# The last w_up tiles of each half are turned beside w_down's first row tiles

## The chip, the cores and the metric

The kernel runs on one core of a Trainium2 chip. The metric is the device time of one execution in microseconds. The timed runs of the kernel before gave 1473.55, 1473.86 and 1475.04 us.

## The reference, cut to what matters

One hybrid decoder layer on 256 tokens of width 2048, in float32. Its first part (a state-space group and an attention group behind one input projection, then an output projection) isn't touched here. The change lies in the last part, the MLP:

```
hdn = jax.nn.relu(jnp.einsum('bsd,df->bsf', u, w_up))          # u 256 x 2048, w_up 2048 x 8192
ff  = jnp.einsum('bsf,fd->bsd', hdn * hdn, w_down)             # w_down 8192 x 2048
out = h + rmsnorm(ff, norm_mlp_post)
```

## The kernel before, in words

**Halves.** The hidden width of 8192 is worked in two halves of 4096 features. Each half is made by products with w_up, column blocks of 512, two at a time (`unit(w_ups[hf], fb, ...)`), and then used as the contraction of w_down, again two column blocks of 512 at a time: `unit(w_down, 0, ...)` and `unit(w_down, 2, ...)` for half 0, the same with `w_downs[1]` for half 1. The partial sums of half 0 stay in three tiles `mw0`, `mw1`, `mw2`.

**A matrix product.** Float32 values are split in two, a rounded part `hi` (ScalarE, `split`, L148) and the rest `lo` (VectorE, L149), and a product takes three matmuls: hi x hi, hi x lo, lo x hi. `row_tiles` does this for one row tile k, 256 rows of the weight, and one column block; both blocks together take 24 matmuls. `seven` does both blocks at once for one k with seven products in place of eight, 21 matmuls, with sums of weights (`e`, `r`, L255, made by VectorE from the two raw tiles) and sums of activations (`sums_of_acts`, L394 to L397 and a split). The sums of activations of a k are made once, kept in two places of `room["sums"]` and used again by the second unit of the half. Which k goes by seven and in which order is a table (`plan`): for the first unit of half 0 the order is 0, 1, 2, 4, 3, 6, 5, 9, 7, 10, 8, 11, 12, 13 with sevens at 4, 6, 9, 10, 11, 13, and then 14 and 15; for the first unit of half 1 the first seven is k = 3.

**Turning.** The result of w_up has tokens on partitions, and w_down needs features there. At the end of each w_up unit four tiles (two blocks by two token tiles) are turned by the generator `turned`: ScalarE squares the tile (L1477) and parts its 32-bit words into 16-bit halves in `ha` (L1478), SyncE issues a DMA transpose of the halves (L1479), and after two steps of waiting ScalarE puts the halves together again (L1482) and the result is split into the activations `ah`, `al` (L148, L149). The generators wait in `beside`; `pump_beside` carries the next one a step on, once after each row tile and twice after each seven, and `drain_beside` runs all to their end. The last four turned tiles of a half are the features of w_down's k = 12 to 15.

**Memory.** Four names of the pool `hp` are used in turn: `ha` (six places of 128 x 512), `hb` (two), `wpost` (two) and `mw`. While w_up runs, `ha` holds the four tiles of 16-bit halves and a raw place, `hb` and `wpost` the results that are turned. `beside_down` gives `ha`, `hb`, `wpost` and, last, `mw1` to the sums of w_down's half 0, and `mw2` to a raw weight tile (`room["raw"]`, behind a ring of four raw tiles). In half 1 `ha` becomes three raw places behind the ring and two in `uc`, and `hb` two more places of sums; the first sums lie in `ua`. A new tile of a name may be written only when the last user of the old one is done.

**What sets the order.** The program is written as one sequence. A scheduler places each engine's instructions at build time by the program's order, by blocks of high priority (weights, splits and sums have one), by explicit lines (`split_in_line`) and by its own reckoning of when operands are ready. Each engine then runs its list strictly in order, SyncE's list of DMA issues included, so an instruction that waits holds all behind it. Pairs of rows are added on the way by DMAs that POOL issues (`pair`, L282, L283), four pairs ahead.

In this kernel the w_up loop of a half ends with `drain_beside()`, and only then come `beside_down()` (half 0) or `in_place_of_u()` and the new raw places (half 1), and the first w_down unit.

## Time and profile before

| what | value |
|---|---|
| timed runs, median | 1473.86 us (1473.55 to 1475.04) |
| the profiled execution, its own time | 1469.89 us |
| its span, first to last instruction | 1468.1 us |
| granted TensorE clock, mean over the span | 0.989 |
| TensorE, VectorE, ScalarE, POOL busy | 98%, 88%, 68%, 11% |
| DMA | 340.30 MB, 232 GB/s |

Times in the profile are microseconds from the start of the span. PE is TensorE, DVE is VectorE, ACT is ScalarE, SP (SPq its queue) is SyncE. A line such as L148 is that of the helper which issued the instruction, so the tiles' names tell more than the lines: `hi<-raw` is the split of a raw weight tile, `ah<-ha` that of a turned tile, `ha<-r` (in w_down) that of a sum of activations. A matmul's shown duration runs to its modelled end; from start to start they are closer. `ps` and `acc` are accumulators, `sh`, `sl` and `ah`, `al` the split activations.

### The profile page before, as it was taken

Reading aid. Unit: us, or ns where it says so; the run is one execution under the profiler, and the core shown is the slowest. Engines: PE = TensorE matmul, PEld = TensorE weight load, DVE = VectorE, ACT = ScalarE, POOL = GpSimd, SP = SyncE. Lnnn points to the kernel's source line nnn. Section 1 sums busy time; section 2 is a strip of 40 time slices with the busy share of each in tenths; the row PEclk is TensorE's granted clock in tenths of the full one; section 3 lists DMA queues with packets and bytes.
Section 4 is the critical chain, followed back from the end, with each engine's and each line's share of the span. In section 5 each row is a group of like instructions: output and inputs, shape, how many; then the busy total and the mean of one; then the engine's idle time right before and its main releaser. Section 6 shows DMA issues by size and latency. Waiting matters only on the chain.

```text
span 1468.1 us, 20247 instructions
## 1 busy us (share of the span) xinstructions
PE 1441.2 (98%) x6930; PEld 1209.3 (82%) x6930; DVE 1299.2 (88%) x1881; ACT 1000.9 (68%) x1407; POOL 162.4 (11%) x244
## 2 busy tenths in 40 slices
PE   9999999999999999999999999979999999979998
PEld 8888888888888888888888888858888888858886
DVE  7788888988999787699989999879889999959998
ACT  7577669675666666566666699766565898866564
POOL 0201210121111000011100111000111111101000
PEclk9999999999999999999999999989999999989999
DMA  8967666756898657688867899778888999989854
GB/s 268 281 200 223 187 184 186 230 178 193 236 265 231 186 144 229 216 248 270 266 198 236 250 312 276 192 193 240 253 250 256 262 284 264 268 206 314 240 192 164
DMA packets 201926, 340.30 MB, mean 232 GB/s; under 512 B 45616, under 2 KB 48544, under 8 KB 201824
## 3 DMA queue, kind: packets, MB, share of 16 engines
q1 hardware_dynamic: 174304, 279.72, 60.8%
q0 software_dynamic: 19648, 45.63, 15.3%
q10 hardware_dynamic: 7872, 13.68, 2.8%
q8 instruction: 54, 0.88, 0.2%
q14 instruction: 48, 0.39, 0.1%
HBM read 327.39 MB, written 49.84 MB: 257 GB/s over the span
## 4 chain that ended last, share of the span: by engine, by line
PE 69%; DMA 3%; ACT 3%; DVE 2%; issue 1%; SPq 0%; ACTq 0%; DVEq 0%
PE acc L347 9%; PE acc L349 9%; PE acc L348 9%; PE acc L435 6%; PE acc L436 6%; PE acc L437 6%; PE acc L504 4%; PE ps L347 3%; PE ps L348 3%; PE ps L349 3%; PE ps L437 2%; PE ps L436 2%; PE ps L435 2%; PE acc L507 2%; DMA hb<-ha 1%; DMA raw<-in_w_down_dram 1%
## 5 line engine op out<-in xcount | busy, mean ns | idle before, releaser
L149 DVE TENSOR_TENSOR lo<-raw,hi 128x1024 fp32r<-128x1024 f32 (+1 forms) x402 | 486.8, 1217 | 82.1 <-ACT hi L148 80.2
L148 ACT ACTIVATE hi<-raw 128x1024 fp32r<-128x1024 f32 (+1 forms) x402 | 419.4, 1049 | 199.2 <-PE acc L349 62.2
L504 PE MATMUL acc<-ua,hi 128*128 128x512 f32 x520 | 141.2, 401 | 0.0
L148 ACT ACTIVATE hi<-e 128x1024 fp32r<-128x1024 f32 x66 | 69.8, 1058 | 49.0 <-DVE e L255 41.1
L504 PEld LDWEIGHTS acc<-ua,hi 128*128 128x128 f32 x520 | 91.3, 189 | 14.0
L347 PE MATMUL acc<-hi,ua 128*128 128x512 f32 x228 | 90.1, 395 | 0.0
L348 PE MATMUL acc<-lo,ua 128*128 128x512 f32 x228 | 89.3, 391 | 0.0
L349 PE MATMUL acc<-hi,ua 128*128 128x512 f32 x228 | 89.1, 391 | 0.0
L347 PE MATMUL acc<-hi,sh 128*128 128x512 f32 x220 | 86.5, 395 | 0.0
L349 PE MATMUL acc<-hi,sl 128*128 128x512 f32 x220 | 85.8, 390 | 0.0
L348 PE MATMUL acc<-lo,sh 128*128 128x512 f32 x220 | 85.7, 389 | 0.0
L149 DVE TENSOR_TENSOR lo<-e,hi 128x1024 fp32r<-128x1024 f32 x66 | 80.4, 1219 | 3.8 <-ACT hi L148 3.2
L507 PEld LDWEIGHTS acc<-ua,lo 128*128 128x128 f32 x520 | 76.5, 190 | 8.9
L507 PE MATMUL acc<-ua,lo 128*128 128x256 f32 x520 | 78.8, 281 | 0.0
L436 PE MATMUL acc<-lo,ah 128*128 128x512 f32 x180 | 70.3, 390 | 0.0
L437 PE MATMUL acc<-hi,al 128*128 128x512 f32 x180 | 70.1, 389 | 0.0
L435 PE MATMUL acc<-hi,ah 128*128 128x512 f32 x180 | 70.1, 389 | 0.0
L504 PE MATMUL acc<-uc,hi 128*128 128x512 f32 x208 | 61.4, 405 | 0.0
L435 PE MATMUL acc<-hi,ua 128*128 128x512 f32 x137 | 53.3, 399 | 2.5 <-ACT hi L148 2.5
L436 PE MATMUL acc<-lo,ua 128*128 128x512 f32 x137 | 53.7, 392 | 0.0
L437 PE MATMUL acc<-hi,ua 128*128 128x512 f32 x137 | 53.6, 391 | 0.0
L149 DVE TENSOR_TENSOR lo<-r,hi 128x512 fp32r<-128x512 f32 x66 | 45.2, 684 | 7.9 <-ACT hi L148 7.6
(566 smaller groups left out, 3716.7 us busy)
## 6 DMA issues: line engine op xcount, KB each, us to landing
raw<-in_w_in_dram SPq DMA_DIRECT2D x154, 512.0 KB, 4.4
raw<-in_w_up_dram SPq DMA_DIRECT2D x77, 512.0 KB, 4.8
raw<-in_w_down_dram SPq DMA_DIRECT2D x69, 512.0 KB, 5.3
raw<-in_w_out_dram SPq DMA_DIRECT2D x38, 512.0 KB, 5.1
raw<-pair SPq DMA_DIRECT2D x60, 256.0 KB, 4.2
pair<-in_w_up_dram POOLq DMA_DIRECT2D x56, 256.0 KB, 5.6
pair<-in_w_down_dram POOLq DMA_DIRECT2D x52, 256.0 KB, 6.0
pair<-in_w_in_dram POOLq DMA_DIRECT2D x42, 256.0 KB, 5.8
```

The costliest lines, as they stand in the source:

```text
L148: return (nc.scalar.activation(hi, src, AF.Copy), nc.vector.tensor_tensor(lo, src, hi.bitcast(F32), op=ALU.subtract))
L149: nc.vector.tensor_tensor(lo, src, hi.bitcast(F32), op=ALU.subtract))
L347: nc.tensor.matmul(dst[:, cs], a_h[:, r, ts], hi[:, j, cs], start=begin and j == 0, stop=False)
L348: nc.tensor.matmul(dst[:, cs], a_h[:, r, ts], lo[:, j, cs], start=False, stop=False)
L349: product[t] = nc.tensor.matmul(dst[:, cs], a_l[:, r, ts], hi[:, j, cs], start=False, stop=end and j == KB - 1)
L435: nc.tensor.matmul(dst, a_h, hi[:, j], start=own and first, stop=False)
L436: nc.tensor.matmul(dst, a_h, lo[:, j], start=False, stop=False)
L437: nc.tensor.matmul(dst, a_l, hi[:, j], start=False, stop=own and last)
L504: nc.tensor.matmul(acc[f], hi[:, j, f * P:(f + 1) * P], u(k0 + j), start=k0 + j == 0, stop=False, skip_group_check=True)
L507: nc.tensor.matmul(acc[f][:, 0], lo[:, j, f * P:(f + 1) * P], u(k0 + j)[:, 0], start=False, stop=k0 + j == NK - 1, skip_group_check=True)
```

## The change

In both halves the `drain_beside()` between the w_up loop and w_down is gone. In half 0 `beside_down` now takes only `mw1`, whose two places become the first two of `room["sums"]`, and `mw2`. The rest of the memory (`ha`, `hb`, `wpost`) is taken in `more_beside_down`, which first drains, and which `unit` calls (`ready`) just before its first seven. In half 1 the same is done by `more_in_place`: drain, `ha` and `hb`, and the loads of two post-norm weights. A row tile steps `beside` on twice instead of once (`room["pace"]`) until `beside_up` sets it back to one. What each sum is kept in moves on by two places: k = 4 in `mw1`, k = 6, 9, 10 in `ha`, 11 in `hb`, 13 in `wpost`, and the sums of k = 8, made in the second unit, in `mw1` again where they were in `ha`.

```diff
--- before.py
+++ after.py
@@ -199,18 +199,23 @@
         a = hp.tile([P, 3 * KB, NB], F32, name="ha")
         room["halves"] = [a[:, i].bitcast(U16) for i in range(2 * NT)]
         room["raw"], room["turn"], room["acts"], room["chain"] = [*raws, a[:, 2 * NT:]], turn, act_u, True
+        room["pace"] = 1
         sums_of.clear()
 
     def beside_down():
 
+        m = new_mw(1, F32R)
+        room["sums"] = [m[:, t].rearrange("p (b s) -> p b s", b=2) for t in range(NT)]
+        room["raw"], room["turn"], room["acts"], room["pace"] = [mws[2]], 0, part, 2
+        sums_of.clear()
+
+    def more_beside_down():
+
+        drain_beside()
         a = hp.tile([P, 3 * KB, 2, S], F32R, name="ha")
         b = hp.tile([P, KB, 2, S], F32R, name="hb")
-        room["sums"] = [a[:, k] for k in range(3 * KB)] + [b[:, k] for k in range(KB)]
+        room["sums"] += [a[:, k] for k in range(3 * KB)] + [b[:, k] for k in range(KB)]
         room["sums"] += [hp.tile([P, 2, S], F32R, name="wpost", bufs=2) for _ in range(2)]
-        m = new_mw(1, F32R)
-        room["sums"] += [m[:, t].rearrange("p (b s) -> p b s", b=2) for t in range(NT)]
-        room["raw"], room["turn"], room["acts"] = [mws[2]], 0, part
-        sums_of.clear()
 
     def fetch_next(src, k0, c0, pair=None):
 
@@ -369,7 +374,7 @@
                 if at == n - 1 and at_end:
                     at_end(t, acc[t])
             pump(pumps)
-            pump_beside()
+            pump_beside(room.get("pace", 1))
 
     def gemm_tokens(src, c0, acts, nk, lag=0, at_end=None, pumps=1):
 
@@ -1506,11 +1511,10 @@
             unit(w_ups[hf], fb, orders[("up", hf), fb], (7,), acc, more,
                  lambda x: combine_new(room["shared"], x), 0, (up_end(fb, 0), up_end(fb + 1, 1)))
             acc, more = more, acc
-        drain_beside()
         if hf == 0:
             beside_down()
             unit(w_down, 0, orders[("down", 0), 0], (14, 15), acc, more,
-                 lambda x: combine_new(in_mw(0), x), 0, (onto(0), onto(1)))
+                 lambda x: combine_new(in_mw(0), x), 0, (onto(0), onto(1)), ready=more_beside_down)
             room["raw"], room["turn"] = [new_mw(2)], 0
             room["sums"] += room["sums"][:4]
             unit(w_down, 2, orders[("down", 0), 2], (12, 14, 15), more, acc,
@@ -1527,15 +1531,20 @@
         return at_end
 
     in_place_of_u()
-    a, b = hp.tile([P, 3 * KB, NB], F32, name="ha"), hp.tile([P, KB, 2, S], F32R, name="hb")
     in_u = room["raw"]
-    room["raw"] = [*in_u, *(a[:, k:k + KB] for k in range(0, 3 * KB, KB))]
-    room["sums"] += [b[:, k] for k in range(KB)]
-    room["chain"] = True
-    for n in range(2):
-        load_wpost(norm_mlp_post, n)
+    room["chain"], room["pace"] = True, 2
+
+    def more_in_place():
+
+        drain_beside()
+        a, b = hp.tile([P, 3 * KB, NB], F32, name="ha"), hp.tile([P, KB, 2, S], F32R, name="hb")
+        room["raw"] = [*in_u, *(a[:, k:k + KB] for k in range(0, 3 * KB, KB))]
+        room["sums"] += [b[:, k] for k in range(KB)]
+        for n in range(2):
+            load_wpost(norm_mlp_post, n)
+
     unit(w_downs[1], 0, orders[("down", 1), 0], (14, 15), acc, more,
-         lambda x: combine_onto(0, x), 0, (complete(0), complete(1)))
+         lambda x: combine_onto(0, x), 0, (complete(0), complete(1)), ready=more_in_place)
     room["chain"] = False
 
     def onto_and_h(more):
```

The lines of code after the first hunk are 5 higher in the new kernel, those from the MLP's last part on up to 9. In half 1 no engine's list changes. Three places in half 0:

TensorE at the first seven of w_down, before. `hi_9262`, `hi_9267`, `hi_9271` and `hi_9275` are the four split weight tiles of k = 4, `hi_9310` and `hi_9327` those of row tile 3, `hi_9354`, `hi_9359`, `hi_9363`, `hi_9367` those of k = 6; the numbers tell instances of a name apart.

```order
L437 MATMUL ps_8013<-hi_9262,sl_80 128x512
L435 MATMUL ps_8015<-hi_9275,sh_79 128x512
L436 MATMUL ps_8015<-lo_9276,sh_79 128x512
L437 MATMUL ps_8015<-hi_9275,sl_80 128x512
L347 MATMUL ps_8013<-hi_9310,sh_79 128x512
L347 MATMUL ps_8015<-hi_9310,sh_79 128x512
...
L437 MATMUL ps_8013<-hi_9354,sl_80 128x512
L435 MATMUL acc_8010<-hi_9267,ha_9131 128x512
L436 MATMUL acc_8010<-lo_9268,ha_9131 128x512
L437 MATMUL acc_8010<-hi_9267,ha_9131 128x512
```

And now:

```order
L442 MATMUL ps_8013<-hi_9262,sl_80 128x512
L440 MATMUL acc_8010<-hi_9267,mw1_9113 128x512
L441 MATMUL acc_8010<-lo_9268,mw1_9113 128x512
...
L442 MATMUL acc_8014<-hi_9271,mw1_9113 128x512
L440 MATMUL ps_8015<-hi_9275,sh_79 128x512
L441 MATMUL ps_8015<-lo_9276,sh_79 128x512
L442 MATMUL ps_8015<-hi_9275,sl_80 128x512
L352 MATMUL ps_8013<-hi_9310,sh_79 128x512
...
L440 MATMUL ps_8015<-hi_9367,sh_79 128x512
L441 MATMUL ps_8015<-lo_9368,sh_79 128x512
L440 MATMUL acc_8010<-hi_9359,ha_9247 128x512
L441 MATMUL acc_8010<-lo_9360,ha_9247 128x512
```

The 12 matmuls of k = 4 on its sums stood behind row tile 3 and the first matmuls of k = 6, and read `ha`. They now read `mw1` and come right after the first six of k = 4. The first matmuls that read `ha` are those of k = 6.

ScalarE at the same place, before:

```order
L148 ACTIVATE hi_9271<-raw_9255 128x1024
L1482 ACTIVATE ha_7892<-hb_7889 128x2x512 x2
L148 ACTIVATE hi_9275<-r_9259 128x512
L148 ACTIVATE ah1_3798<-ha_7892 128x4x128 x2
L1482 ACTIVATE ha_7892<-wpost_7890 128x2x512
L1482 ACTIVATE ha_7892<-wpost_7891 128x2x512
L148 ACTIVATE hi_9310<-raw_9308 128x1024
L148 ACTIVATE hi_9327<-mw2_6211 128x1024
L148 ACTIVATE hi_9354<-raw_9343 128x1024
L148 ACTIVATE ah1_3798<-ha_7892 128x4x128 x2
L148 ACTIVATE hi_9359<-e_9350 128x1024
L148 ACTIVATE hi_9363<-raw_9347 128x1024
```

And now:

```order
L1483 ACTIVATE ha_7892<-wpost_7891 128x1024
L148 ACTIVATE hi_9271<-raw_9255 128x1024
L1487 ACTIVATE ha_7892<-hb_7889 128x2x512 x2
L148 ACTIVATE hi_9275<-r_9259 128x512
L148 ACTIVATE ah1_3798<-ha_7892 128x4x128 x2
L1487 ACTIVATE ha_7892<-wpost_7890 128x2x512
L148 ACTIVATE hi_9310<-raw_9308 128x1024
L148 ACTIVATE ah1_3798<-ha_7892 128x4x128
L148 ACTIVATE hi_9327<-mw2_6211 128x1024
L1487 ACTIVATE ha_7892<-wpost_7891 128x2x512
L148 ACTIVATE hi_9354<-raw_9343 128x1024
L148 ACTIVATE ah1_3798<-ha_7892 128x4x128
```

The split of k = 4's sums into `mw1` is new ahead of these rows; the second copy from `wpost` (L1487 now) has moved behind the splits of row tile 3, and the three writes of `ha` in a row are one, later on.

VectorE where the last turned tile is split (`al1`), before:

```order
L255 TENSOR_TENSOR e_9350<-raw_9343,raw_9347 128x512
L149 TENSOR_TENSOR al1_3799<-ha_7892,ah1_3798 128x4x128
L255 TENSOR_TENSOR e_9350<-e_9350,raw_9347 128x512
L149 TENSOR_TENSOR lo_9355<-raw_9343,hi_9354 128x1024
L255 TENSOR_TENSOR r_9351<-e_9350,raw_9343 128x512
L149 TENSOR_TENSOR lo_9360<-e_9350,hi_9359 128x1024
L394 TENSOR_TENSOR r_9392<-ah0_4884,al0_4885 128x512
L149 TENSOR_TENSOR lo_9364<-raw_9347,hi_9363 128x1024
L149 TENSOR_TENSOR al1_3799<-ha_7892,ah1_3798 128x4x128
L149 TENSOR_TENSOR ha_9131<-r_9209,ha_9131 128x512
```

And now:

```order
L260 TENSOR_TENSOR e_9350<-raw_9343,raw_9347 128x512
L260 TENSOR_TENSOR e_9350<-e_9350,raw_9347 128x512
L149 TENSOR_TENSOR lo_9355<-raw_9343,hi_9354 128x1024
L260 TENSOR_TENSOR r_9351<-e_9350,raw_9343 128x512
L149 TENSOR_TENSOR lo_9360<-e_9350,hi_9359 128x1024
L149 TENSOR_TENSOR lo_9364<-raw_9347,hi_9363 128x1024
L149 TENSOR_TENSOR lo_9368<-r_9351,hi_9367 128x512
L399 TENSOR_TENSOR r_9392<-ah0_4884,al0_4885 128x512
L149 TENSOR_TENSOR al1_3799<-ha_7892,ah1_3798 128x4x128
L400 TENSOR_TENSOR r_9393<-r_9392 128x256
L149 TENSOR_TENSOR lo_9403<-raw_9400,hi_9402 128x1024
L149 TENSOR_TENSOR ha_9247<-r_9301,ha_9247 128x512
```

The last `al1` stood behind the low part of `hi_9363`; it now stands behind `lo_9368` as well, and one write of `ha` follows two steps after it.

SyncE's queue, before:

```order
L162 DMA raw_9343<-in_w_down_dram 128x2x512
L1479 DMA_TRANSPOSE hb_7889<-ha_7892 128x8x128 x2
L157 DMA raw_9347<-pair1_90 128x512
L158 DMA raw_9347<-in_w_down_dram 128x512
L1479 DMA_TRANSPOSE wpost_7890<-ha_7892 128x8x128
L1479 DMA_TRANSPOSE wpost_7891<-ha_7892 128x8x128
```

And now:

```order
L162 DMA raw_9343<-in_w_down_dram 128x2x512
L1484 DMA_TRANSPOSE hb_7889<-ha_7892 128x8x128 x2
L1484 DMA_TRANSPOSE wpost_7890<-ha_7892 128x8x128
L157 DMA raw_9347<-pair1_90 128x512
L158 DMA raw_9347<-in_w_down_dram 128x512
L1484 DMA_TRANSPOSE wpost_7891<-ha_7892 128x8x128
```

The first `wpost` transpose has moved ahead of the two loads of k = 6's second block.

## The prediction

> **What bounds the kernel now.** I read the page first, for the span and TensorE's share of it, and then the waits of TensorE, longest first.
>
> ```profile
> span 1468.1 us, 20247 instructions
> PE 1441.2 (98%) x6930; PEld 1209.3 (82%) x6930; DVE 1299.2 (88%) x1881; ACT 1000.9 (68%) x1407; POOL 162.4 (11%) x244
> PE ps L435 <- ACT hi L148: 5.0, 2, 3.7
> PE ps L347 <- ACT hi L148: 4.8, 2, 2.5
> PE acc L435 <- ACT hi L148: 4.4, 2, 2.5
> PE acc L435 <- ACT ha L148: 3.8, 1, 3.8
> ```
>
> TensorE is busy 98% of the span. Its four largest waits (total, times, longest) add up to 18.0 us, and none of them is for an idle resource: each is for a ScalarE split. Busy time by stretch (stretch, length, then PE, PEld, DVE, ACT, POOL, granted clock, DMA share, GB/s) places them: one stall begins after 953 us, where w_down begins in the first half, another at 1300, where it begins in the second half, and between them TensorE has no gap.
>
> ```profile
> 960.00:980.00 20.00, 14.56 (x49) 11.26 (x50) 14.44 (x20) 11.20 (x14) 2.16 (x3) 0.77 0.66 169
> 980.00:1000.00 20.00, 20.00 (x90) 16.58 (x89) 19.71 (x27) 11.62 (x13) 1.36 (x2) 1.00 0.75 223
> 1000.00:1020.00 20.00, 20.00 (x90) 16.57 (x89) 19.08 (x25) 12.45 (x16) 2.72 (x4) 1.00 0.84 244
> 1300.00:1320.00 20.00, 11.35 (x33) 7.43 (x32) 9.62 (x13) 11.76 (x16) 0.55 (x1) 0.76 0.69 194
> ```
>
> The timeline of TensorE through the first stall (start, duration, engine, line, operands, and in brackets the idle time and its releaser):
>
> ```profile
> 953.05 0.39 PE L437 MATMUL ps<-hi,sl 128*128 128x512 f32 x1
> 957.18 0.79 PE L435 MATMUL ps<-hi,sh 128*128 128x512 f32 x1 [3.74 <-ACT hi L148]
> 961.66 1.22 PE L347 MATMUL ps<-hi,sh 128*128 128x512 f32 x2 [2.54 <-ACT hi L148]
> 973.09 0.80 PE L435 MATMUL acc<-hi,ha 128*128 128x512 f32 x1 [3.78 <-ACT ha L148]
> 982.03 0.39 PE L347 MATMUL ps<-hi,sh 128*128 128x512 f32 x1
> 987.48 0.39 PE L435 MATMUL acc<-hi,ah 128*128 128x512 f32 x1
> ```
>
> By the order of instructions 953.28 to 987.48 holds 84 matmuls: 3 left of the seven of k = 4, its 12 on sums, 24 of row tile 3, 6 + 12 + 3 of the seven of k = 6, and 24 of row tile 5. The last 24 run from 982.03 to 987.48, 0.227 us each. At that rate 84 take 19.1 us; they take 34.2. So 15.1 us are lost, 10.1 of them in the three waits and 5.0 to a lower granted clock (0.77 in that stretch) after them.
>
> **What the waits are for.** ScalarE and SyncE's queue at that place (the last row is the page's, with the median us to landing):
>
> ```profile
> 946.19 5.69 SPq L1479 DMA_TRANSPOSE hb<-ha  x2
> 952.05 0.46 SPq L157 DMA_DIRECT2D raw<-pair  x1
> 953.08 3.86 SPq L1479 DMA_TRANSPOSE wpost<-ha  x2
> 947.33 1.04 ACT L1478 ACTIVATE ha<-wpost 128x1024 uint16<-128x1024 uint16 x1
> 952.95 1.35 ACT L1482 ACTIVATE ha<-hb 128x1024 uint16<-128x1024 uint16 x1 [1.73 <-DMA hb<-ha]
> 955.31 1.34 ACT L1482 ACTIVATE ha<-hb 128x1024 uint16<-128x1024 uint16 x1 [1.01 <-DMA hb<-ha]
> 956.52 0.60 ACT L148 ACTIVATE hi<-r 128x512 fp32r<-128x512 f32 x1
> 957.03 1.13 ACT L148 ACTIVATE ah<-ha 128x512 fp32r<-128x512 f32 x2
> 958.17 2.54 ACT L1482 ACTIVATE ha<-wpost 128x1024 uint16<-128x1024 uint16 x2
> 960.58 1.03 ACT L148 ACTIVATE hi<-raw 128x1024 fp32r<-128x1024 f32 x1
> 972.41 1.15 ACT L148 ACTIVATE ha<-r 128x512 fp32r<-128x512 f32 x2 [1.95 <-DVE al L149]
> raw<-pair SPq DMA_DIRECT2D x60, 256.0 KB, 4.2
> ```
>
> Wait one (3.74 us): the split of the sum weights `hi<-r` stands behind two copies that wait for the transposes. Wait two: the split of row tile 3 stands behind four more steps of the drain, the last two 2.54 us together. Wait three: the sums of k = 4 live in `ha`, which is free only when the last `al<-ha` of the drain is done.
>
> **The change, part by part.** *The first sums move to `mw1`.* Its 12 matmuls now stand ahead of wait one, and need nothing of the drain. They fill 953.28 + 12 x 0.227 = 956.0. `hi<-r` itself does not move: the two `hb` transposes still land where they did, so TensorE restarts at 957.18, after 1.2 us instead of 3.9. Its price on ScalarE is one 128x512 split (0.60) ahead of the `wpost` copies, which falls into the 1.73 us in which ScalarE waits for the transposes; on VectorE its 0.6 us falls into the wait for `hi<-r`. Both hide there, and would cost 0.6 us of wait one without it.
>
> *One `wpost` copy goes behind the split of row tile 3.* That split starts 1.2 us earlier (half of 2.54, the pair being pipelined), at 959.4, and TensorE has it at 960.45 instead of 961.66. *On SyncE* one transpose passes the two loads of k = 6's second block: it starts at 952.05, not 953.08, and the loads go 1.3 us later (of the 3.86 on two transposes the first takes a third). At 4.2 us from issue to landing they are there by 958, and VectorE reads them first at 963.9; nothing waits. A transpose that reaches the head of the queue before its copy on ScalarE is done would hold every load behind it, but that copy (947.33, now 0.5 later) is done at 949.
>
> *The third wait.* No longer the sums of k = 4 but those of k = 6 wait for `ha`, and the last `al` stands further back on VectorE. Rows for its steps:
>
> ```profile
> 963.92 0.69 DVE L255 TENSOR_TENSOR e<-raw 128x512 f32<-128x512 f32 x1
> 964.52 0.68 DVE L149 TENSOR_TENSOR al<-ha,ah 128x512 fp32r<-128x512 f32 x1
> 982.40 1.22 DVE L149 TENSOR_TENSOR lo<-mw,hi 128x1024 fp32r<-128x1024 f32 x1
> 983.53 0.68 DVE L255 TENSOR_TENSOR r<-e,mw 128x512 f32<-128x512 f32 x1
> ```
>
> From start to start a 128x1024 step costs 1.13 and a 128x512 step 0.60. From the split at 960.45 VectorE has five of the first kind and seven of the second up to and with the last `al` (the two `e` and the sums' subtraction included): 5.7 + 4.2 + 0.1 for one dependent pair = 10.0, so 970.45. The write of `ha` on ScalarE (0.63) gives 971.2. Is TensorE there by then? The second half has had this very order all along, so its rows tell how TensorE gets through row tile 4:
>
> ```profile
> 1301.72 0.51 PE L435 MATMUL ps<-hi,sh 128*128 128x512 f32 x1 [1.31 <-ACT hi L148]
> 1305.42 0.80 PE L347 MATMUL ps<-hi,sh 128*128 128x512 f32 x1 [2.23 <-ACT hi L148]
> 1306.68 0.80 PE L348 MATMUL ps<-lo,sh 128*128 128x512 f32 x1 [0.46 <-DVE lo L149]
> 1310.59 0.40 PE L348 MATMUL ps<-lo,sh 128*128 128x512 f32 x1
> 1313.58 0.39 PE L349 MATMUL acc<-hi,sl 128*128 128x512 f32 x1
> ```
>
> There 24 matmuls take 1305.42 to 1313.81, 8.4 us, the nine from 1306.68 on at 0.43 each. So TensorE ends row tile 3 at 968.85, runs 8 more matmuls of k = 6 until 970.65, waits 0.55 us for `ha` (3.78 before), does 12 + 1 until 974.15 and row tile 5 until 979.6. Before it was 987.48. **The gain is 7.9 us.** At full clock TensorE would only reach the same wait earlier (960.45 + 1.25 for `lo` + 31 x 0.227 = 968.7), so the sum does not hang on the clock's return.
>
> *The end of the half.* `mw1` now holds the sums of k = 8, the last seven of the second unit, so `combine_new` may write there only after that seven. Rows for it:
>
> ```profile
> 1096.13 0.58 ACT L444 ACTIVATE mw<-ps 128x512 f32<-128x512 f32 x1
> 1098.83 0.68 DVE L445 TENSOR_TENSOR r<-mw,ps 128x512 f32<-128x512 f32 x1
> 1115.99 0.39 PE L347 MATMUL ps<-hi,ua 128*128 128x512 f32 x1
> ```
>
> In the new order three splits stand ahead of that copy; it starts about 4 us later, VectorE follows by 2.5 us, and TensorE needs these banks only at 1115.99. That costs nothing.
>
> *The second half.* Every engine's order from `in_place_of_u` on, and its waits, are those of before: the loads up to the first seven come into the same places by the short list as by the long one, and the drain was already spread among the row tiles' steps. Gain 0; the stall at 1300 stays.
>
> **Bounds.** From below: at half clock right up to `ha` (1.25 + 31 x 0.43 from 960.45, so 975.0, then 37 x 0.227) the end is 983.4 and the gain 4.1. From above: full clock and no wait for `ha` gives 968.7 + 37 x 0.227 = 977.1, gain 10.4. I keep 7.9, the case that the second half's rows show. VectorE's lead is the other unknown: before, k = 9's `lo` (982.40) was done 3.9 us ahead of its use at 987.48; now the last `al` (970.45) is followed by three steps (2.1 us) through the low half of `ha`, 972.5, and seven more (4.6) through this `lo`, 977.1, for use at 979.6: a lead of 2.5. From there both engines need about 10.2 us for a pair of a row tile and a seven (45 x 0.227), so the lead holds.
>
> **Rivals.** (1) *VectorE becomes the bound* at k = 9. For: 19.71 us busy of 20 in 980 to 1000. Against: 19.08 and no wait of TensorE in the next stretch, and sums that are now interleaved, so that dependent steps don't stall. It gives back 2 to 4 us: gain 4 to 6, 1468 to 1470. (2) *The gain is swallowed later*, if the loads and not TensorE set the pace after 987. For: DMA share 0.75 to 0.84. Against: TensorE 20.00 of 20 there, which loads behind their time would not allow. Time 1473.9, no change. (3) *The clock stays down*: TensorE restarts in short bursts with waits of 1.2 and 2 us and one for `lo` between them. At 0.43 from 960.45 through row tile 5 the end is 975.0 + 37 x 0.43 = 990.9, 3.4 us later than before: 1477.3. It decides once 20 of these last 37 matmuls are slow ((987.48 - 983.4) / 0.203). Against: 1310.59 is back at full speed after the same pattern. [...] (4) *The second half gains too*, if the loads into `ha` behind its drain came earlier: the waits of 4.4 us above (`acc L435 <- ACT hi`, both there) and 7.9 make 12.3, 1461.6. Against: the same order there.
>
> **How the numbers follow.** The sum stands against the profiled execution, 1469.89 us (span 1468.1): 1462.0. The median of the timed runs is 1473.86, 4.0 above; I carry the difference in us over: 1473.86 - 7.9 = 1466.0. The chances: forecast (gain 6 to 10.4) 0.73, rival 1 0.13, rival 2 0.08, rival 3 0.04, rival 4 0.02. About 0.2%, 2.9 us, can be told from no change. Faster: 0.73 + 0.13 + 0.02 = 0.88; same 0.08; slower 0.04. The range goes from the upper bound (1463.4) over rival 1 (1470.2), which leaves out 0.14.
>
> **What would show it.** In the new profile TensorE's waits should read: one of about 1.2 us at `ps<-hi,sh` (L440) after the 12 matmuls on `mw`, one of about 2 at row tile 3, one under 1.5 at `acc<-hi,ha`, and the same three of the second half. The stretch 980 to 1000 should have no wait. Wrong would be: a wait over 2 us at `ha`, TensorE waiting for `lo` at k = 9 or 10, a granted clock under 0.8 past row tile 5, or a second half with another order of waits.

## The result, and the profile after

| kernel | median | range | runs |
|---|---|---|---|
| before | 1473.55 us | 1470.51 to 1475.04 | 5 |
| changed | 1460.71 us | 1458.87 to 1464.47 | 5 |

The ratio is 0.9922 (95% interval 0.9901 to 0.9943): 12.8 us between the medians, 8.4 to 14.6 by the interval. The forecast was 1466.0 (1463.4 to 1470.2), faster: the sign was right, and the time lies below the range. The profiled execution of the changed kernel took 1458.87 us, with a span of 1457.1 us against 1468.1, a granted clock of 0.995 against 0.989, and the same number of matmuls. One later run of the kernel before took 4496.13 us and is left out of every median and range below. TensorE's waits, longest first (total, times, longest):

```profile
PE 1436.0 (99%) x6930; PEld 1205.5 (83%) x6930; DVE 1296.9 (89%) x1881; ACT 1000.9 (69%) x1407; POOL 162.6 (11%) x244
PE acc L440 <- ACT hi L148: 6.2, 2, 3.2
PE ps L352 <- ACT hi L148: 3.1, 2, 1.7
PE ps L440 <- ACT hi L148: 1.7, 1, 1.7
PE ps L353 <- DVE lo L149: 1.2, 2, 0.8
```

These four are 12.2 us in all, where the four largest before made 18.0. The 3.8 us for `ha` are gone, and of two waits at a seven's `ps` (L435, now L440) one is left; those at `acc` (6.2 against 4.4, both in the second half) and for `lo` (1.2 against 0.5) are longer. By stretch (PE, PEld, DVE, ACT, POOL, granted clock, DMA share, GB/s):

```profile
960.00:980.00 20.00, 18.61 (x68) 14.52 (x69) 19.03 (x25) 14.42 (x17) 2.17 (x3) 0.83 0.80 230
980.00:1000.00 20.00, 20.00 (x90) 16.57 (x89) 19.92 (x29) 12.94 (x14) 1.95 (x4) 1.00 0.86 251
```

In 960 to 980 TensorE is busy for 18.61 us (14.56 before), and 980 to 1000 has no gap. TensorE through the first stall:

```profile
951.79 0.39 PE L440 MATMUL acc<-hi,sh 128*128 128x512 f32 x1
957.74 0.50 PE L440 MATMUL ps<-hi,sh 128*128 128x512 f32 x1 [1.70 <-ACT hi L148]
960.92 0.79 PE L352 MATMUL ps<-hi,sh 128*128 128x512 f32 x1 [1.72 <-ACT hi L148]
962.18 0.79 PE L353 MATMUL ps<-lo,sh 128*128 128x512 f32 x1 [0.47 <-DVE lo L149]
967.04 0.55 PE L352 MATMUL acc<-hi,sh 128*128 128x512 f32 x1
971.78 0.50 PE L440 MATMUL acc<-hi,ha 128*128 128x512 f32 x1
980.37 0.39 PE L440 MATMUL acc<-hi,ah 128*128 128x512 f32 x1
```

The seven of k = 4 begins at 951.79 and the first seven on turned tiles, k = 9, at 980.37: 28.58 us. Before, the same matmuls ran from 951.91 to 987.48, 35.57 us. I call these 28.58 and 35.57 the *first stall* from here on. Its three waits are 1.70, 1.72 and none, where they were 3.74, 2.54 and 3.78. What they wait for, on ScalarE and (the last two rows) VectorE:

```profile
934.49 1.06 ACT L148 ACTIVATE hi<-raw 128x1024 fp32r<-128x1024 f32 x1 [2.53 <-DMA raw<-in_w_down_dram]
937.73 1.06 ACT L148 ACTIVATE hi<-raw 128x1024 fp32r<-128x1024 f32 x1 [2.18 <-DMA raw<-in_w_down_dram]
938.69 1.32 ACT L1475 ACTIVATE hb<-hb,rmlp 128x512 f32<-128x512 f32 x2
954.66 2.55 ACT L1487 ACTIVATE ha<-hb 128x1024 uint16<-128x1024 uint16 x2 [2.28 <-DMA hb<-ha]
957.08 0.60 ACT L148 ACTIVATE hi<-r 128x512 fp32r<-128x512 f32 x1
971.10 0.63 ACT L148 ACTIVATE ha<-r 128x512 fp32r<-128x512 f32 x1
...
970.32 0.68 DVE L149 TENSOR_TENSOR al<-ha,ah 128x512 fp32r<-128x512 f32 x1
976.46 1.22 DVE L149 TENSOR_TENSOR lo<-mw,hi 128x1024 fp32r<-128x1024 f32 x1
```

By *the drain* I mean the steps that still have to be done on the last four turned tiles. It is a chain that begins behind two splits of w_down's rows, which wait for their loads: the first step on a turned tile at 938.69, the transposes back at 954.66, the last `al<-ha` at 970.32, and the first sum written into the drain's place, `ha<-r`, at 971.10.

The rest of the difference is in the second half, where no engine's list has changed. From the first seven (k = 3) to the first product on turned tiles I call it the *second stall*:

```profile
1296.17 0.39 PE L435 MATMUL acc<-hi,sh 128*128 128x512 f32 x1
1315.87 0.50 PE L435 MATMUL acc<-hi,sh 128*128 128x512 f32 x1 [1.90 <-ACT hi L148]
1319.12 0.80 PE L435 MATMUL acc<-hi,ua 128*128 128x512 f32 x1 [2.52 <-ACT hi L148]
1326.82 0.39 PE L435 MATMUL acc<-hi,ah 128*128 128x512 f32 x1
```

```profile
1288.72 0.39 PE L440 MATMUL acc<-hi,sh 128*128 128x512 f32 x1
1295.03 0.49 PE L352 MATMUL ps<-hi,sh 128*128 128x512 f32 x1 [1.39 <-ACT hi L148]
1305.02 0.60 PE L440 MATMUL acc<-hi,sh 128*128 128x512 f32 x1 [3.19 <-ACT hi L148]
1309.06 0.80 PE L440 MATMUL acc<-hi,ua 128*128 128x512 f32 x1 [3.01 <-ACT hi L148]
1315.80 0.39 PE L440 MATMUL acc<-hi,ah 128*128 128x512 f32 x1
```

30.65 us before (the first rows), 27.08 now. Its last wait, at `acc<-hi,ua`, ends 22.95 us after the first seven before and 20.34 now. From the end of the first stall the two executions run 7.1 us apart, and 7.45 where this stall begins.

### The profile page after: what moved, and what is told of

It reads as the page before. It is cut to its first block, busy times and chain, and to the rows that moved or that the text cites. A ratio compares the mean times of both kernels' runs of the same rounds, so it can differ in the third digit from the quotient of the medians.

```text
span 1457.1 us, 20248 instructions
## 1 busy us (share of the span) xinstructions
PE 1436.0 (99%) x6930; PEld 1205.5 (83%) x6930; DVE 1296.9 (89%) x1881; ACT 1000.9 (69%) x1407; POOL 162.6 (11%) x244
## 4 chain that ended last, share of the span: by engine, by line
PE 69%; ACT 3%; DVE 2%; DMA 2%; issue 1%; SPq 0%; ACTq 0%; DVEq 0%
PE acc L352 9%; PE acc L354 9%; PE acc L353 9%; PE acc L440 6%; PE acc L442 6%; PE acc L441 6%; PE acc L509 4%; PE ps L353 3%; PE ps L354 3%; PE ps L352 3%; PE ps L442 2%; PE ps L441 2%; PE ps L440 2%; PE acc L512 2%; DVE lo L149 1%
## 5 line engine op out<-in xcount | busy, mean ns | idle before, releaser
L440 PE MATMUL acc<-hi,ah 128*128 128x512 f32 x180 | 70.0, 389 | 0.0
L440 PE MATMUL acc<-hi,ua 128*128 128x512 f32 x137 | 52.9, 396 | 3.0 <-ACT hi L148 3.0
L148 ACT ACTIVATE hi<-r 128x512 fp32r<-128x512 f32 x66 | 41.1, 623 | 14.6 <-PE acc L354 8.2
```

The source lines that it names most:

```text
L148: return (nc.scalar.activation(hi, src, AF.Copy), nc.vector.tensor_tensor(lo, src, hi.bitcast(F32), op=ALU.subtract))
L440: nc.tensor.matmul(dst, a_h, hi[:, j], start=own and first, stop=False)
```

## The experiments

Eight kernels were run beside the kernel before, and the kernels before and changed were run again. All stalls below are measured as above, in each kernel's own trace. `relu` is the start of the drain's first step on ScalarE and `ha` that of the first write into the drain's place, both counted from the first matmul of the first seven of half 0.

| kernel | median us | first stall | relu | ha | second stall |
|---|---|---|---|---|---|
| before | 1473.55 | 35.57 | -13.86 | 20.50 | 30.65 |
| second half's edit alone | 1471.47 | 34.07 | -14.96 | 18.97 | 29.84 |
| before, again | 1469.24 (one run) | 36.58 | -13.20 | 21.25 | 28.31 |
| before, a third time | 1471.57 (one run) | 37.72 | -13.74 | 21.25 | 28.89 |
| changed | 1460.71 | 28.58 | -13.10 | 19.31 | 27.08 |
| sums' places alone | 1461.2 | 28.32 | -13.47 | 19.10 | 27.89 |
| changed, again | 1460.63 | 28.94 | -13.05 | 19.72 | 27.08 |
| changed, a third time | 1458.60 (one run) | 27.78 | -14.23 | 18.55 | 26.73 |
| added matmuls of zeros | 1463.1 | 27.81 | -14.24 | 17.88 | 27.87 |
| `ha` late in the raw ring | 1461.77 | 25.91 | -15.54 | 16.70 | other order |
| one more row tile ahead | 1461.43 | other order | | | 28.25 |
| drain first | 1455.65 | 22.65 | -17.92 | 13.67 | 27.86 |
| drain first, all of it | 1456.93 | 24.45 | -17.32 | 13.87 | 28.99 |
| before, drain first | 1467.23 | 34.36 | -16.27 | 19.27 | 28.43 |

### Which part of the change does it

The second half's edit alone, in the kernel before:

```diff
+    room["chain"], room["pace"] = True, 2
+    def more_in_place():
+        drain_beside()
+        a, b = hp.tile([P, 3 * KB, NB], F32, name="ha"), hp.tile(...)
...
-         lambda x: combine_onto(0, x), 0, (complete(0), complete(1)))
+         lambda x: combine_onto(0, x), 0, (complete(0), complete(1)), ready=more_in_place)
```

> Edit: the kernel before with the change's edit of half 1 alone (the drain, `ha`, `hb` and the two post-norm loads taken at the first seven, two steps of turning per row tile in that unit). Every engine's list of instructions and waits is that of the kernel before. Theory 1 (the gain comes from half 0's order alone; what the second half of the profile gained, 30.65 against 27.08 us from the first seven's first matmul to the first matmul on `ah`, is spread between executions): ratio to before 1.000, between 0.998 and 1.002, and in its trace 28.6 us in half 0 is not reached: about 35.6 there; the second half anywhere between 26 and 31. Theory 2 (half 1's edit gives 3 to 5 us of the gain): ratio 0.997 or lower, second half near 27.

1471.47 us, ratio 1.0009 (0.9996 to 1.0022). Its instruction lists are those of the kernel before on every engine, and so is its time.

The places of the sums alone. The kernel before, with the drain, the pace and half 1 as they were:

```diff
     def beside_down():
+        m = new_mw(1, F32R)
+        room["sums"] = [m[:, t].rearrange("p (b s) -> p b s", b=2) for t in range(NT)]
         a = hp.tile([P, 3 * KB, 2, S], F32R, name="ha")
         b = hp.tile([P, KB, 2, S], F32R, name="hb")
-        room["sums"] = [a[:, k] for k in range(3 * KB)] + [b[:, k] for k in range(KB)]
+        room["sums"] += [a[:, k] for k in range(3 * KB)] + [b[:, k] for k in range(KB)]
...
-        m = new_mw(1, F32R)
-        room["sums"] += [m[:, t].rearrange("p (b s) -> p b s", b=2) for t in range(NT)]
```

> Edit: the kernel before with one thing changed: `beside_down` takes `mw1` first and makes its two places the first two of the sums; the drain, the pace and all of half 1 stay as before. Theory 1 (the place of the first sums does all of it; the moved drain moves no instruction): the same lists as the changed kernel, so its time, ratio 0.992 (0.990 to 0.995), about 28.6 us from the first seven of w_down to k = 9 in half 0. Rival (turning beside the row tiles gives a part): ratio 0.996 or higher and over 31 us there. For the second half: if its 27.1 us followed from everything coming 7 us earlier, this trace has 27 again; if it is spread, anything from 26 to 31.

1461.2 us, ratio 0.9940 (0.9927 to 0.9953), with a first stall of 28.32. Its lists are those of the changed kernel on every engine, waits included. So the swap of places is the whole change: the sums of k = 4 need a place that the drain does not hold. That the turning is written beside the row tiles moves nothing; the scheduler had it there already.

### What sets the first stall

One more row tile ahead of the first seven, and the order behind it to match (changed kernel):

```diff
-            plan(("down", 0), w_down, 0, (0,1,2,4,3,6,5,9,7,10,8,11,12,13), (4,6,9,10,11,13))
+            plan(("down", 0), w_down, 0, (0,1,2,3,4,5,6,7,9,8,10,12,11,13), (4,6,9,10,11,13))
```

> Edit: the changed kernel with row tile 3 of w_down's first unit in half 0 ahead of the first seven (order 0, 1, 2, 3, 4, 5, 6, 7, 9, 8, 10, 12, 11, 13, the same sevens). Theory 1 (what is left of half 0's stall, 28.6 us for 84 matmuls of 19.1 us, is one chain from the transposes' landing through ScalarE and VectorE to `ha`; 24 more matmuls ahead of the seven cover 5.4 us of it): from k = 2's end to k = 9 some 4 to 6 us less than the changed kernel, ratio to before 0.987 to 0.990. Rival (ScalarE's and VectorE's own work sets the pace there, so moving a row tile moves the wait behind it): ratio 0.991 to 0.994, the same sum of waits at other places.

1461.43 us, ratio 0.9947 (0.9934 to 0.9960): the changed kernel's time; the 4 to 6 us of the theory did not come. The matmuls that were ahead of k = 9 now end at 979.44 (984.89 less 5.45 for row tile 7, which has come ahead of it too), 27.92 us after row tile 2 (951.52), where the changed kernel's traces take 27.78 to 28.94. The waiting has only moved behind row tile 3, as the rival had it: ScalarE waits 5.57 us for the first transpose, until 957.13, and the splits of the seven stand behind it. In this order `ha` is not the limit; it is written at 967.61, 8 us ahead of its first use.

The raw places in `ha` join the ring of half 1 from the 17th load on only (changed kernel):

```diff
+        if "later" in room and room["turn"] == 12:
+            room["raw"], room["turn"] = room.pop("later"), 6
...
-        room["raw"] = [*in_u, *(a[:, k:k + KB] for k in range(0, 3 * KB, KB))]
+        room["later"] = [*in_u, *(a[:, k:k + KB] for k in range(0, 3 * KB, KB))]
```

> Edit: the changed kernel, and in half 1 the three raw places in `ha` join the ring only at the 17th load of the unit, so that k = 6 and k = 5 are loaded into the ring and not behind the drain. The waits for a load into `ha` cost 3.19 + 3.01 us in the changed kernel's second half (1.90 + 2.52 before) and slow matmuls after them. Theory 1 (these loads are that half's largest part): the second half's stretch goes from 27 to 31 us to 21 to 23, ratio to before 0.987 to 0.990. Rival (the five loads that now stand ahead of the transposes on SyncE's queue hold the transposes up, and ScalarE with them): waits of 3 us or more at the first seven's last product and at row tile 4, stretch 27 or more, ratio 0.992 or higher.

1461.77 us, ratio 0.9951 (0.9938 to 0.9964), no better than the changed kernel, as the rival had it. In the second half the loads no longer wait for the drain, but they now stand ahead of the drain's transposes on SyncE's queue, which go out 2.4 us after the first seven where they went 8.6 us before it (1280.14 in the changed kernel, whose first seven is at 1288.72). SyncE's row of the changed kernel, and then SyncE's and two waits of TensorE here:

```profile
1280.14 5.73 SPq L1484 DMA_TRANSPOSE hb<-ha  x2
```

```profile
1289.55 7.99 SPq L1486 DMA_TRANSPOSE hb<-ha  x2
...
1301.01 0.80 PE L354 MATMUL acc<-hi,sh 128*128 128x512 f32 x1 [5.25 <-ACT hi L148]
1326.56 0.83 PE L354 MATMUL ps<-hi,sh 128*128 128x512 f32 x2 [4.51 <-ACT hi L148]
```

This run's first half, whose order is the changed kernel's, told more than the edit:

```profile
951.91 0.39 PE L442 MATMUL acc<-hi,sh 128*128 128x512 f32 x1
969.29 0.50 PE L442 MATMUL acc<-hi,ha 128*128 128x512 f32 x1 [1.43 <-ACT ha L148]
977.82 0.39 PE L442 MATMUL acc<-hi,ah 128*128 128x512 f32 x1
```

25.91 us, at full clock throughout (1.00 in 940 to 960 and in 960 to 980), with a wait of 1.43 for `ha`. Two readings were left: the clock had cost the others 2.6 us (an estimate: 13 matmuls at 0.43 and not at 0.227), or the drain had simply ended 2.6 us earlier (`ha` 16.70 us after the first seven, 19.31 in the changed kernel). To tell them apart, twelve matmuls on a stationary operand of zeros were put into the two waits of the changed kernel, to see whether the clock then stays up:

```diff
+            if dst is acc[2] and room.get("keep"):
+                for _ in range(6):
+                    nc.tensor.matmul(dst[:80], zeros, hl_b[0][:, 0], start=False, stop=False)
...
+        if room.pop("keep", False):
+            for _ in range(6):
+                nc.tensor.matmul(acc[2][:80], zeros, hl_t[0][:, 0], start=False, stop=False)
```

> The changed kernel with twelve more matmuls in the first half, with a stationary operand of zeros (128x80), which add nothing to the sums: six ahead of the first seven's last three, six behind them, 1.4 us each at full clock, in the two waits of 1.70 and 1.72 us. They take the dip of the granted clock away (0.83 in 960 to 980) and leave the drain as it is. By the prediction the sum does not hang on the clock: TensorE then only comes earlier to the wait for the drain's place (about 1.5 to 2.5 us of wait there), the stretch from the first seven to k = 9 stays at 27.9 to 28.7 us, and the time is that of the changed kernel within 1 us. Rival: the 13 matmuls at 0.43 (2.6 us) are on the path, and the stretch falls to 25.5 to 26.5, the time by 2 to 2.6 us. A small loss, up to 1 us, if the added matmuls outlast the waits.

The stretch of 960 to 980, and TensorE at both ends and at the wait:

```profile
960.00:980.00 20.00, 16.79 (x70) 13.03 (x71) 18.98 (x25) 13.20 (x16) 2.16 (x3) 1.00 0.65 192
```

```profile
951.97 0.39 PE L444 MATMUL acc<-hi,sh 128*128 128x512 f32 x1
970.53 0.51 PE L444 MATMUL acc<-hi,ha 128*128 128x512 f32 x1 [2.46 <-ACT ha L148]
979.78 0.39 PE L444 MATMUL acc<-hi,ah 128*128 128x512 f32 x1
```

The clock is 1.00 (0.83 in the changed kernel), and the first stall takes 27.81 us against 27.78 to 28.94: TensorE is early at `ha` and waits 2.46 us there. The time, 1463.1 us (ratio 0.9953, 0.9934 to 0.9971), is 2.5 above the changed kernel's 1460.63 beside it and not below, more than the 1 us that was allowed for; where that goes, no run shows. The edit also did more than it was meant to: the scheduler moved steps of VectorE and ScalarE from 967 on, and two matmuls that stood ahead of `ha` now stand behind it; the stall is `ha` plus 9.93 here.

The run with `ha` late is the cleaner witness, since its first half has the changed kernel's order and ran at full clock. In it and in the four runs of the changed order (a clock of 0.88 over the stall) the first stall is `ha` plus 9.21 to 9.27 us (28.58 - 19.31, 28.32 - 19.10 and so on), and `ha` comes 32.2 to 32.8 us after `relu`. VectorE tells why: from row tile 3's split to the last `al` it has no gap over 0.15 us in the changed kernel. So `ha` is on the path, as the prediction had it, and the slow matmuls ahead of it cost next to nothing. They are close to it, though. In the third trace of the changed kernel the split ahead of `ha<-r` waited for TensorE,

```profile
969.88 1.06 ACT L148 ACTIVATE hi<-raw 128x1024 fp32r<-128x1024 f32 x1 [2.58 <-PE acc L354]
```

and `ha<-r` started at 970.85, some 0.35 us later than the last `al` (done at 970.39) would have let it.

### What sets the drain

Then the drain's start should be worth its full size. In the changed kernel it stands at 938.69 behind the two splits at 934.49 and 937.73, with 2.53 and 2.18 us of waiting for loads. Two edges put the first column block's steps ahead of such splits, in both halves:

```diff
+    def first_of_turning():
+        square, copy = zip(*room["steps"])
+        room["first"] = [(), (), (), square, copy]
...
             if fetch is fetch_next:
+                with ExitStack() as order:
+                    for step in room["first"].pop(0) if room.get("first") else ():
+                        order.enter_context(tc.issue_after(step[0].ins))
                     split_in_line(hi, lo, raw)
```

> The changed kernel, with two edges for order on ScalarE in each half: the fourth split of w_down's rows (second column block of row tile 1) is queued behind the squares of the turned tiles of the first column block, and the fifth behind their copies. Nothing else is changed; the transposes then stand ahead of the last two loads on SyncE's queue by themselves. Theory: both stalls hang on when the drain starts, and that hangs on splits of w_down's rows that wait for their loads on ScalarE (2.53 and 2.18 us in the profile of the changed kernel, at 934.49 and 937.73) with the first step of the drain queued behind them, though its operand is there by 934.6. Freed of them the copies end 4 to 5 us earlier, the transposes land 4 us earlier, so the first half's stretch from the first seven to k = 9 falls from 28.6 to 21 to 24 us (90 matmuls of 0.227 are 20.4), the second half's from 27.1 to 28.3 to 22 to 25, and the time falls by 8 to 12 us, to 1449 to 1453. Rival 1: the transposes' own time or DMA share sets the landing (they queue behind loads that are under way): gain 0 to 3 us. Rival 2: the splits that now stand further back make TensorE wait for row tile 1's second block (needed at 943.75, its split 1.7 us later): gain 4 to 8 us, with a wait at ps or acc for hi before the first seven.

1455.65 us, ratio 0.9907 (0.9888 to 0.9926), 5.0 us below the changed kernel beside it (six runs each, 1453.98 to 1459.48 and 1456.92 to 1462.74): the fastest here, though the two ratios' intervals still touch. ScalarE, SyncE's queue and TensorE in the first half:

```profile
932.88 1.06 ACT L148 ACTIVATE hi<-raw 128x1024 fp32r<-128x1024 f32 x1 [1.83 <-DMA raw<-in_w_down_dram]
933.84 0.71 ACT L1478 ACTIVATE hb<-hb,rmlp 128x512 f32<-128x512 f32 x1
936.80 1.24 SPq L1495 DMA_TRANSPOSE hb<-ha  x1
940.44 1.25 SPq L1495 DMA_TRANSPOSE hb<-ha  x1
951.76 0.39 PE L443 MATMUL acc<-hi,sh 128*128 128x512 f32 x1
966.11 0.50 PE L443 MATMUL acc<-hi,ha 128*128 128x512 f32 x1 [1.19 <-ACT ha L148]
974.41 0.39 PE L443 MATMUL acc<-hi,ah 128*128 128x512 f32 x1
```

The drain starts at 933.84. Of the two waits for splits the second (2.18) is gone from ahead of it and the first is still there, 1.83 at 932.88. `ha` comes 13.7 us after the first seven and the first stall takes 22.65 us (90 matmuls at 0.227 us each would take 20.4). The theory's 21 to 24 holds there; its time, 1449 to 1453, was not reached. In the second half it fell: the transposes went out 4 us earlier, and the copies that come back then stood behind two splits of the seven,

```profile
1281.18 1.06 ACT L148 ACTIVATE hi<-e 128x1024 fp32r<-128x1024 f32 x1 [1.51 <-DVE e L260]
1284.04 2.57 ACT L1498 ACTIVATE ha<-hb 128x1024 uint16<-128x1024 uint16 x2
```

and the second stall stayed at 27.86. Two more edges free those copies (the seven's first split goes behind the second column block's copies, its third behind the first block's return):

```diff
+            copy, back = room.pop("seven", ((), ()))
+            with ExitStack() as order:
+                for step in copy:
+                    order.enter_context(tc.issue_after(step[0].ins))
+                split_in_line(*hl_a, raw_a)
...
+            with ExitStack() as order:
+                for step in back:
+                    order.enter_context(tc.issue_after(step[0].ins))
+                split_in_line(*hl_b, raw_b)
```

> The changed kernel with the two edges of the earlier drain and two more on ScalarE in each half: the first split of the first seven is queued behind the copies of the turned tiles of the second column block, and its third behind the copies that come back from the first column block's transposes. With the two edges alone the first half's stretch fell to 22.65 us (20.4 is full speed), but the second half's stayed at 27.86: the transposes went out 4 us earlier there, and then the copies that come back stood behind the seven's splits (at 1284.04, behind one that waited 1.51 us for the first sum), and the second column block's copy started at 1282.15. Theory: in the second half what counts is when the whole drain ends, since the loads into its place follow that; freed of these splits it ends 2 to 4 us earlier, and the stretch falls to 24 to 26 us; the first half's to 21 to 22.7; the time by 2 to 4 us against the kernel with two edges, to 1451.5 to 1454. Rival: the second half's stretch is set by the landing of the loads into the drain's place and the transposes queue behind other loads: no change, 1455 to 1456. It would be worse, by 1 to 2 us, if the seven's third split now comes too late for TensorE.

1456.93 us, ratio 0.9910 (0.9894 to 0.9925): no gain, as the rival said. The second stall was 28.99, and the drain's last `al` there came 10.1 us after the first seven, where it came 10.7 with two edges and 9.7 to 11.2 in the changed kernel's three traces. The last transpose landed 4.6 us after the first seven, 4.1 with two edges and 4.1 to 5.7 in those three: the second column block's transposes came back no earlier, and why is not settled.

The first stall was 24.45, where 21 to 22.7 was expected. `ha` came as with two edges (13.87 against 13.67), but after the wait for it TensorE ran at half speed (rows of TensorE and of the window behind it):

```profile
966.68 0.50 PE L450 MATMUL acc<-hi,ha 128*128 128x512 f32 x1 [1.20 <-ACT ha L148]
967.30:970.70 3.40, 3.40 (x10) 2.63 (x9) 3.37 (x7) 1.85 (x3) 0.00 (x0) 0.50 1.02 351
```

Eight matmuls there, at about 0.43 from start to start and not 0.227, cost 1.6 us more, and the stall is `ha` plus 10.59, 1.6 more than with two edges (8.98). TensorE waits for nothing more behind `ha` in this stall, so the dip of the clock counts in full here.

The same two edges in the kernel before, where the sums of k = 4 still lie in the drain's place:

> The kernel before (sums of k = 4 in the drain's place, no swap) with the same two edges on ScalarE. Theory: with the drain 4 us earlier the swap has little left to gain: here TensorE still meets the wait for the sums of k = 4 in the drain's place, but 4 us earlier than in the kernel before, 0 to 3 us of it, so the time is 1450 to 1456, 14 to 19 us below the kernel before and 0 to 3 above the changed kernel with the same edges. Rival: the swap's 8 us and the earlier drain's gain are separate and add up: 1457 to 1461 here.

```profile
953.59 0.39 PE L438 MATMUL acc<-hi,sh 128*128 128x512 f32 x1
962.01 1.22 PE L350 MATMUL ps<-hi,sh 128*128 128x512 f32 x2 [5.41 <-ACT hi L148]
973.54 0.80 PE L438 MATMUL acc<-hi,ha 128*128 128x512 f32 x1 [3.78 <-ACT ha L148]
987.95 0.39 PE L438 MATMUL acc<-hi,ah 128*128 128x512 f32 x1
```

1467.23 us, ratio 0.9978 (0.9962 to 0.9995), 11.6 us above the changed kernel with these edges. Both expectations fell. The drain starts 2.4 us earlier than in the kernel before, but its last `al` still comes at 18.5 us, so `ha` is written at 19.3: in this order the last two splits of turned tiles stand behind those of row tile 3 and the first of k = 6 on ScalarE, and TensorE waits 5.41 us for row tile 3 and 3.78 for `ha`. The same edges were worth 5.0 us with the swap and 3.3 without it.

### How large the gain is

The changed kernel and the kernel before, unchanged:

> The changed kernel as it is, again, to settle the size. The prediction's gain of 7.9 us was right, and the rest of the 12.8 us between the two medians was a slow spell of the kernel before (its median was 1473.55 beside the changed kernel and 1469.84 beside the four kernels of the first experiments, while the kernels with the swap stood at 1460.7 and 1461.2): then the ratio here is 0.994 (0.9935 to 0.9945, so 8 to 9.5 us). Rival: the second half's stall gains 3 us with the swap each time, and the ratio is 0.992 (0.9915 to 0.993, 10.5 to 12.5 us). In its trace the stretch from the first seven's first matmul to that of k = 9 in the first half takes 28 to 29 us by both (35.57 before); the second half's from the first seven to the first product on the turned tiles takes 28.5 to 30 by the first (30.65 before, 29.84 in the kernel with the second half's edit alone), 27 to 28.3 by the second (27.08, 27.89 and 28.25 in three kernels with the swap).

> The kernel before once more, for the spread of its two stalls from run to run. Measured so far, from the first seven's first matmul to that of k = 9 in the first half: 35.57 and 34.07 us with this instruction order, 28.58, 28.32 and 28.94 with the swap. From the first seven to the first product on the turned tiles in the second half, where both kernels have one order: 30.65 and 29.84 without the swap, 27.08, 27.89, 28.25, 27.08 and 27.87 with it. If the second half gains with the swap each time, this run shows 29.5 to 31 there; if that was spread (28.43 without the swap in the kernel with the two edges speaks for it), it may as well show 27 to 29.

> The same kernel a third time, for the same question: 29.5 to 31 us in the second half's stretch if the swap gains there each time, 27 to 31 if it is spread. In the first half 34 to 36 us by both.

> The changed kernel a third time: 27 to 28.3 us in the second half's stretch if the swap gains there each time, up to 31 if it is spread. In the first half 28 to 29.5 us by both.

The changed kernel again: 1460.63 us, ratio 0.9936 (0.9917 to 0.9956). Its median has been 1460.71 and 1460.63, and 1461.2 for the same lists; the kernel before had 1473.86 in the three runs the forecast started from, and 1469.84, 1470.50 and 1470.36 over 17, 22 and 10 runs beside these experiments, single runs from 1465.5 to 1477.4. By the table's means the first stall takes 35.99 us in four traces without the swap and 28.41 in four with it, 7.6 less. The second stall takes 28.31 to 30.65 (mean 29.42) in those four and 26.73 to 28.25 (27.48) in the six traces whose first half has the swap and whose second half has the order of both, 1.9 less. Together 9.5 us, and 1470.4 - 9.5 = 1460.9.

So neither reading of the first expectation holds alone: the ratio is nearer to that of the first, and the second stall is that of the second. Nor did the kernel before show the 29.5 to 31 us that were expected if the second half gains each time: its two new traces had 28.31 and 28.89, so a good part of the 3.57 us of the first pair was spread, and 1.9 is what the means leave. Most of what the forecast missed was its base, the three runs of the kernel before, and about 2 us are the second half.

## Why the prediction was right or wrong, point by point

**What the waits were for: right.** All three waits belong to the drain, and the swap takes the sums of k = 4 out of it.

**The first sums move, and a `wpost` copy goes behind the split: right, with the first wait 0.5 us longer in this profile.** TensorE came to the last three matmuls of k = 4 at 957.74 (957.18 foreseen) after 1.70 us, because the first transpose came back at 954.66 and not at 952.95; over four traces this wait was 0.59 to 2.11. The wait at row tile 3 was 1.72 (about 2 foreseen), and TensorE began row tile 3 at 960.92 (960.45 foreseen).

**The third wait: right in what sets it, 0.6 us late.** From row tile 3's split to the last `al` VectorE took 10.1 us (10.0 foreseen), so `ha` was ready for TensorE at 971.78 and not at 971.2: the 0.5 us of the first wait, handed on. TensorE hardly waited for it (0.55 foreseen), since the slow stretch on the way held 13 matmuls, 10 of them 0.43 from start to start, and not 9. That the two still met is luck; with all of them slow TensorE itself would have come last, at 975.0 by the estimate in the forecast's lower bound. K = 9 began at 980.37 (979.6 foreseen). The gain of the first stall is 6.99 us between the two profiled executions and 7.6 over the eight traces, against 7.9.

**"The sum does not hang on the clock's return": right to within 0.35 us,** by the run with `ha` late, the one with matmuls of zeros and the third trace above. The windows around the slow part, of the changed kernel and then of the kernel before:

```profile
960.50:967.40 6.90, 6.01 (x13) 4.42 (x14) 6.46 (x8) 6.63 (x9) 0.81 (x1) 0.51 0.74 197
```

```profile
955.40:965.70 10.30, 5.98 (x12) 3.85 (x13) 5.95 (x8) 9.13 (x11) 1.36 (x2) 0.50 0.90 188
```

The clock was 0.51 over 6.9 us and 0.50 over 10.3 us, after waits of 1.70 and 1.72 us and of 3.74 us; in the 6.8 us on either side of both windows it was 1.00. The length of a wait alone does not tell when this comes. Slow matmuls (0.43 from start to start) also followed waits of 0.97 and 0.76 us in the run with one more row tile ahead, and one of 1.20 in the run with all of the drain first; none followed one of 1.59 in the run with `ha` late or one of 2.46 in the run with matmuls of zeros. What sets it off, and what sets whether 9 or 13 matmuls are slow, the traces do not show.

**Rivals 1 to 3: rightly low.** VectorE's `lo` for k = 9 started at 976.46 and was done 2.7 us ahead of its use (2.5 foreseen), 980 to 1000 has no wait, nothing was given back later, and the clock was at 1.00 again from 967.4. The nine slow matmuls that the forecast reads in the trace of before are not its longest run of them: some eleven stand behind the wait at 1319.12.

**The end of the half: right.** TensorE has no wait between 962.18 and 1295.03.

**"The second half. Gain 0; the stall at 1300 stays": wrong by about 2 us.** The step's ground, that every engine's order and waits there are those of before, is true, and the stall does stay. Yet it was shorter in all six traces with the swap than in all four without, if only by 0.06 us at the nearest. Between the two profiled executions it was 3.57. No instruction explains it, and no run here shows a cause. Rival 4 (the loads into `ha` come earlier there) named the place: with the swap they start 10.4 to 11.9 us after that half's first seven (mean 11.2), without it 11.6 to 13.3 (12.2), which is 1 of the 1.9 us, and the last wait, at `acc<-hi,ua`, ends at 19.5 to 21.1 (20.4) against 21.2 to 23.0 (21.9), which is 1.5. Why they start earlier with the same lists stays open. Rival 4's 4.4 us was too much; that its time, 1461.6, lies nearest to the measured one is luck, since it stands on the high base.

**"I carry the difference in us over: 1473.86 - 7.9": the step that failed.** The profiled execution at 1469.89, which the working had in hand, was the nearer to the kernel's usual time: 49 later runs have their medians at 1469.84 to 1470.5. From 1470.4 the same sum gives 1462.5, 1.8 from the measured 1460.7. The median of three runs was 3.5 us high, and the range gave that no room; carried over to 1470.4 it would have been 1459.9 to 1466.7 and held the result. Of the 5.3 us of error 3.5 are this term and 1.9 the second half. Why the first runs of the kernel before were slower stays open: four of the five took 1473.07 us or more, and of the 49 later ones nine did.

## What to carry to other kernels

A buffer's place in a ring is part of the schedule: here what counted was not when the turning was written, but that the first consumer's operands lay in memory that the turning still held, and moving those operands to a place that it did not hold gave the whole gain. Where a chain of small steps runs through one engine's list, look at what stands ahead of its first step: here two splits that waited 2.53 and 2.18 us for loads, and two edges there were worth another 5 us with the swap, and 3.3 without it. These stalls hang on when transfers land (ScalarE waited 2.28 us for the transposes in the changed kernel), and over four traces of one order the first took 34.07 to 37.72 us and the second 28.31 to 30.65, so a base of three runs that lies 4 us from the profiled one should have widened the range by that much.

## What the runs showed of the hardware that was not expected

The drain's length hardly varies (32.2 to 32.8 us from `relu` to `ha` in the five traces with the changed kernel's order), while its start moves by 2.5 us, behind splits that wait for weight loads; with it the first stall moves from 25.9 to 28.9 us.

Half speed of TensorE cost next to nothing where it fell ahead of a wait for another chain (10 to 12 slow matmuls in the changed kernel's traces, none in the run with `ha` late, and `ha` plus 9.2 us in all), and its full 1.6 us where it fell behind the last wait.

The issue of a transpose on SyncE's queue took 1.24 us where it stood by itself in the rows of 936.80 and 940.44 above (2.38 for one by itself at 949.30 in the same run) and 2.85 and 2.79 where two stood together behind loads (the pair at 946.19 in the kernel before). In the changed kernel the same pair took 2.14 and 4.46, and the second half's first pair took 5.7 to 8.7 us in all, but 1.24 each where the early drain had set them apart. Why they take longer there, the traces do not show.
